# A hybrid encoder block on one core: every work buffer at a multiple of 512 bytes

## The chip, the cores and the metric

The kernel runs on one core of a Trainium2 chip. Times are device microseconds (us) of one execution. The kernel before took 1132.4 us (median of three runs, 1129.93 to 1132.73).

## What is computed

One layer over 1024 rows of 1024 numbers, all float32:

```
h = rmsnorm(x, norm1_g)
q, k, v, u = split(h @ w_in)
a = attention_mixer(q, k, v, ...)          # 8 query heads, 2 key heads, 2-D rotary positions
p = pool_mixer(u, ...)                     # four groups of 128 channels, windows 2, 4, 8, 16:
                                           #   window mean of u minus u, then a 128x128 map
x = x + concat([a, p]) @ w_out
h = rmsnorm(x, norm2_g)
x = x + (silu(h @ w_gate) * (h @ w_up)) @ w_down     # inner width 2816
```

## The kernel before

Each float32 operand of a product is split into a rounded part and the rest (`hi`, `lo`, type float32r), and a product is three passes on TensorE: hi·hi, hi·lo, lo·hi. A pass is one weight load of 128x128 (the stationary operand) and one matmul in which up to 512 columns (2048 bytes in each partition, the moving operand) stream past it.

The stages follow each other on TensorE: the input projection (line 469 for keys and values, 664 for the pooling groups, 580 for queries), the pooling groups' linear map (722), attention (scores 790, transposes of the weights 820, values 833) with the output projection between (870), then the gate and up products of the feed-forward part (1124), which take Winograd's form (seven block products instead of eight), and in the same form the down product (1397), once after every four blocks of gate and up; the last down product is plain (1349). A gate or up block is 84 matmuls, seven block products of twelve; four blocks are 336.

The order in which all engines issue is fixed before the program is built: class `Flow` plays the program with estimated costs, and a job's instruction is issued when its operands and engine are free by that estimate. Each engine then takes its own list in order. Splits and sums may fall to ScalarE (ACT), VectorE (DVE) or GpSimd (POOL), whichever `Flow.quicker` says is done first.

SBUF is laid out by tile pools, one after another. The pool `wk` has 33 work slots that hold nearly everything: transposed rows, split weights, attention weights, sums. A slot is as large as the largest tile asked of the pool. That is a pooling tile: `windows` (line 678) takes tiles of S + PAD = 1032 numbers, since eight zeros ahead of the 1024 rows of u stand for the rows before the first. So a slot is 4128 bytes, 8 x 512 + 32. In the built program the first slot starts 320 bytes past a multiple of 512, and each next slot 32 bytes further: a work tile's place modulo 512 takes all 16 multiples of 32. Behind `wk` lie `raw` (weights as loaded, 3 slots) and `ring` (split operands, 3 slots), 4096 bytes each, all at 352 modulo 512, and from the other end of SBUF the tiles `vv`, `fold`, `identr` and the pool `half`, at 480. `kT` lies at 352, the rows `qp` at 320, the float32 identity `ident` at 128. In line 1124 the stationary operand is always in `ring` and the moving one in `wk`; in line 1397 the stationary is in `ring`, and the moving one in `raw` for most steps and in `wk` for some.

The pooling window sums are made by doubling on DVE (lines 687, 690), then the mean minus u (696) and the first and last rows, whose windows are cut, apart (702, 704).

Of the kernel before, what the change touches and what calls it, by code (L numbers as in the profile page):

```python
# [41 lines left out]
AHEAD = 2  # L42
NSLOT = 33
NRAW = 3
K = {
    "pieces": 1, "groups": [[0], [1], [2, 3], [4, 5, 6, 7]], "take": [0, 3], "tables": 2, "spread": [1],
    "ahead": [22, 39], "turn_k": 40, "wq": [60], "mix": [40, 50, 0, 15], "prep_q": [20], "turn_q": [33],
# [54 lines left out]


class Nothing:
    """Stands for the machine where only the order of the work is sought."""

    def __getattr__(self, name):
        return self
# [26 lines left out]


class Flow:
    """Fixes the order in which the engines issue their instructions.

    The tensor engine's instructions come in the order of the program.  Work of the other  # L140
    engines is given as generators that yield (engine, estimated us) before each instruction,
    or a list of jobs to wait for; an instruction is issued when the estimate says that
    its engine and its operands are free by the time the tensor engine gets there."""

    LATENCY = 0.15
    COLD = 12.0
# [87 lines left out]
        held[held.index(None)] = job  # L234

    def needs(self):
        """When the tensor engine, never held up, would ask for each job."""
        for job in reversed(self.all):
            for other, before in job.waits:
                other.need = min(other.need, job.need - (job.cost - before))  # L240
        return [job.need - job.cost for job in self.all]
# [30 lines left out]
def block_kernel(  # L272
# [14 lines left out]
    pairs = ExitStack()  # L287
    ps2 = pairs.enter_context(tc.tile_pool(name="ps2", bufs=2, space=bass.MemoryType.PSUM))

    const = sb(ctx, "const")  # L290
    small = sb(ctx, "small", bufs=2)
    ident = const.tile([P, P], F32, name="ident")
    if not isinstance(nc, Nothing):
# [34 lines left out]
            nc.vector.tensor_tensor(lo, src, hi.bitcast(F32), op=ALU.subtract)  # L328

    def combine(n, dst, a, b, op):  # L330
        """dst = a op b in SBUF on whichever of DVE and Pool is done with it first"""
        way = flow.quicker(dve(n), pool(n))
        yield way
        (nc.gpsimd if way[0] == "G" else nc.vector).tensor_tensor(dst, a, b, op=op)  # L334
# [57 lines left out]
        return hs[a][h][k // 2][:, o:o + n]  # L392

    def load_w(col, n, per, apart=False):
        """W_in[:, col:col+n] as (hi, lo, job) for each k."""
        res = []
        for j in range(NK // per):
            raw, at, tok = fetch(
                lambda v: v.rearrange("p (k n) -> p k n", n=n),
                w_in2[j * per * P:(j + 1) * per * P, col:col + n].rearrange("(k p) n -> p k n", p=P))  # L400
            hi, lo = work(F32R), work(F32R)
            if not apart:
                job = consume(tok, flow.add(split(hi, lo, raw, D, both=True), at))
            for k in range(per):
                c = slice(k * n, (k + 1) * n)
                if apart:
                    job = consume(tok, flow.add(split(hi[:, c], lo[:, c], raw[:, c], n, both=True), at))
                res.append((hi[:, c], lo[:, c], job))
        return res
# [242 lines left out]

    def pool_group(g):
        wu = wus.pop(g)
        u = work(n=S + PAD)
        nc.gpsimd.memset(u[:, 0:PAD], 0.0)
        jobs = []
        for h in range(2):
            pu = bank()
            for k in range(NK):  # L660
                hi, lo, job = wu[k]
                flow.tensor(0.648, job, *[x_turned[t, k] for t in range(4 * h, 4 * h + 4)])
                for i, (a, b) in enumerate(PASSES):
                    nc.tensor.matmul(pu, (hi, lo)[a], hT(b, k, h * HALF, HALF), start=(k == 0 and i == 0), stop=(k == NK - 1 and i == 2))  # L664
                if k < NK - 1:
                    yield

            def evacuate(h, pu):
                yield [rb_jobs[h]]
                yield dve(HALF)  # L670
                nc.vector.tensor_tensor(u[:, PAD + h * HALF:PAD + (h + 1) * HALF], pu, rb[0][:, h * HALF:(h + 1) * HALF], op=ALU.mult)

            jobs.append(flow.add(evacuate(h, pu)))
            flow.hold("b1", jobs[-1])
            if h == 1:
                pooled_parts[g] = flow.add(windows(g, u, jobs))
            yield

    def windows(g, u, jobs):
        w = WINDOWS[g]  # L680
        yield jobs
        n = S + PAD
        ab = [work(n=n), work(n=n)]
        cur, step, i = u, 1, 0
        while step < w:
            yield dve(n)
            nc.vector.tensor_tensor(ab[i][:, 0:n - step], cur[:, 0:n - step], cur[:, step:n], op=ALU.add)
            if 2 * step < w:
                yield dve(1)
                nc.vector.tensor_copy(ab[i][:, n - step:n], cur[:, n - step:n])  # L690
            cur, step, i = ab[i], 2 * step, 1 - i
        hw = w // 2
        off = PAD - hw
        pooled = ab[i][:, 0:S]
        yield dve(S)
        nc.vector.scalar_tensor_tensor(pooled, cur[:, off:off + S], 1.0 / w, u[:, PAD:PAD + S], op0=ALU.mult, op1=ALU.subtract)
        for s, (c0, cn) in enumerate(((0, hw), (S - hw + 1, hw - 1))):
            if cn == 0:
                continue
            ec = small.tile([P, PAD], F32, tag="ec", name="ec")  # L700
            yield dve(1)
            nc.vector.tensor_tensor(ec[:, :cn], cur[:, off + c0:off + c0 + cn], edge[:, g, s, :cn], op=ALU.mult)
            yield dve(1)
            nc.vector.tensor_tensor(pooled[:, c0:c0 + cn], ec[:, :cn], u[:, PAD + c0:PAD + c0 + cn], op=ALU.subtract)
        ph, pl = work(F32R), work(F32R)
        us[g] = ph, pl
        yield from split(ph, pl, pooled, S, both=True)
# [143 lines left out]
    class OutProj:  # L851
# [3 lines left out]
            self.rows = rows  # L855

        def run(self, n):
            """n times the three passes of one k"""
            for _ in range(min(n, NK - self.i)):
                k = KORDER[self.i]  # L860
                if self.i == 0:
# [103 lines left out]
            x2n_job[t0 + i] = flow.add(scaled(first, i))  # L965

    def turn_h(h, k):
        """128 columns of the normalised rows of half h, transposed and split."""
        pt, name = any_bank()
        for i in range(4):  # L970
            flow.tensor(0.107, x2n_job[4 * h + i])
            nc.tensor.transpose(pt[:, i * P:(i + 1) * P], x2n[4 * h + i][:, k * P:(k + 1) * P], ident)
        dst = pieces()

        def evacuate():
            yield act(512, 0.05)
            nc.scalar.activation(dst[:, 0], pt, AF.Copy, scale=g2[:, k:k + 1])
            yield dve(512)
            nc.vector.scalar_tensor_tensor(dst[:, 1], pt, g2[:, k:k + 1], dst[:, 0].bitcast(F32), op0=ALU.mult, op1=ALU.subtract)

        h2[h, k] = dst, flow.add(evacuate())
        return pt, name, h2[h, k][1]
# [8 lines left out]
    t_split = {}  # L991

    def sums_of(i, p12, n12, job12, p22, n22, job22):
        """The sums of both halves' parts i and i + 4 that Winograd's form takes."""
        j = i + PARTS
        t1, t2, t3, t4 = (spare() for _ in range(4))
        a, b = h2[0, i][0], h2[0, j][0]
# [134 lines left out]
    wdown = {}  # L1132

    def fetch_down(f):
        """Rows of w_down for a pair whose last product takes Winograd's form."""
        t = work()
        nc.sync.dma_start(t, w_down2[f * P:(f + 1) * P, :])
        wdown[f] = t, flow.load(P * D * 4, flow.now)

    class Passed:  # L1140
        """Stands in for the reader of a slot that the tensor engine reads."""
        done, ready = False, float("inf")

    made_pair, passed = {}, {}

    def sums(p, name):
        """The sums in place that an operand of pair p needs."""
        made = made_pair.setdefault(p, {})
        if name in made:
            return made[name]  # L1150
# [32 lines left out]
    FORM = {"A11": "B11", "S1": "T1", "A12": "B21", "S2": "T2", "S3": "T3", "S4": "B22", "A22": "T4"}  # L1183

    def make_pair(p, name):
        """Both operands of one of Winograd's products of the last product, for pair p."""
        made = made_pair.setdefault(p, {})
        other = FORM[name]
        left = {"A11": (0, 0), "S1": (1, 0), "A12": (0, 1), "S2": (1, 0), "S3": (0, 0), "S4": (0, 1), "A22": (1, 1)}[name]
# [26 lines left out]
        return (x, jl), (y, jr)  # L1216

    def emit(b, q, psum, name, plus, *waits):
        """Block q of the output, plus + psum, on its way to g; the bank goes back when it is read."""
        kind, p = blocks[b]  # L1220
        f, h = 2 * p + int(q[0]) - 1, int(q[1]) - 1
        if kind == "g":
# [83 lines left out]
        users[:] = [e22, e12, emit(b, "21", b4, n4, u, j4)]  # L1306

    def plain_tile(b, f, h, *fills):
        """Tile f of block b for half h: the operands' numbers, and how many to have ready after each."""
        py, name = any_bank()  # L1310
        for i, (n, fill) in enumerate(fills):
            n, fill = n + b * len(FIRST), fill + b * len(FIRST)
# [40 lines left out]
                    split_wd(2 * p + 1, 1)  # L1353

    def into(t, c, src, op=ALU.add, in_bank=True, last=False, waits=(), n0=0, size=HALF):
        """One more term of the output's tile (t, c)."""
        cs = slice(c * HALF + n0, c * HALF + n0 + size)
        dst = qp[:, t, cs]

# [286 lines left out]
```

## Time and profile before

| | before |
|---|---|
| runs, us | 1132.73, 1132.4, 1129.93 |
| median, us | 1132.4 |
| profiled execution: first to last instruction, us | 1131.3 |
| TensorE (PE) busy, us | 1087.5 |
| weight loads (PEld) busy, us | 880.1 |
| DVE, ACT, POOL busy, us | 875.7, 454.1, 553.0 |
| granted TensorE clock, mean | 0.994 |

The profile gives one execution; its span is its whole time, 1.1 us below the median of the runs. A matmul's own duration (some 395 ns for 512 columns) is longer than the distance from one matmul's start to the next, as they are pipelined; what counts for the time is the distance, which is read from the starts of two rows, or from the chain of waits, where a row's length is the time until the next row and its x the number of matmuls.

### The profile page before, as it was taken

What the parts mean: (1) busy time and instruction counts of PE and PEld (TensorE: products, weight loads), DVE (VectorE), ACT (ScalarE), POOL (GpSimd) and SP (SyncE); (2) the same over time, 40 slices, a digit from 0 to 9 for tenths busy, and PEclk for the clock granted to TensorE, in tenths of its full rate; (3) what the DMA queues carried; (4) which work ended last, traced back from release to release, by engine and by line L of the source; (5) the groups of instructions that cost most, each with busy time, mean ns of one, the idle gap of its engine ahead of it and who ended that gap; (6) DMA issues with size and microseconds to landing.
All of it is one profiled execution on the core that took longest, in us unless ns stands there. A gap on an engine that the chain in (4) does not pass through costs nothing.

```text
span 1131.3 us, 14027 instructions
## 1 busy us (share of the span) xinstructions
PE 1087.5 (96%) x5114; PEld 880.1 (78%) x5114; DVE 875.7 (77%) x1371; ACT 454.1 (40%) x808; POOL 553.0 (49%) x442
## 2 busy tenths in 40 slices
PE   6989998999999999999899999999899989999998
PEld 6868876888888888878678877888688867887787
DVE  7888699977676765887986689658976698668985
ACT  6613367666666554522431233223322232223320
POOL 3163566522333223754862387336843485238820
PEclk9999999999999999999999999999999999999999
DMA  8112011000000001130122002310122012200113
GB/s 257 56 38 75 19 56 38 19 20 19 10 20 17 22 29 56 38 112 1 38 94 75 19 19 75 99 32 1 46 86 93 1 38 92 76 19 10 46 56 149
DMA packets 42565, 58.49 MB, mean 52 GB/s; under 512 B 4224, under 2 KB 32768, under 8 KB 42496
## 3 DMA queue, kind: packets, MB, share of 16 engines
q1 hardware_dynamic: 42496, 57.59, 15.9%
q8 instruction: 40, 0.66, 0.2%
q14 instruction: 29, 0.24, 0.1%
HBM read 53.39 MB, written 4.19 MB: 51 GB/s over the span
## 4 chain that ended last, share of the span: by engine, by line
PE 78%; DVE 15%; POOL 3%; issue 3%; ACT 1%; DMA 0%; SPq 0%; DVEq 0%; ACTq 0%; POOLq 0%
PE b L1124 36%; PE b L1397 8%; PE b L870 8%; PE b L833 5%; PE b L790 5%; PE b L820 5%; DVE wk L334 3%; PE b L664 3%; DVE silu L334 2%; DVE qp L1364 2%; PE b L1349 2%; PE b L580 2%; PE b L469 2%; POOL wk L334 1%; DVE ring L334 1%
## 5 line engine op out<-in xcount | busy, mean ns | idle before, releaser
L1124 PE MATMUL b<-wk,ring 128*128 128x512 f32 x1872 | 437.0, 395 | 1.4 <-DVE ring L321 1.4
L1124 PEld LDWEIGHTS b<-wk,ring 128*128 128x128 f32 x1872 | 351.4, 188 | 85.5 <-DVE ring L321 1.9
L1397 PE MATMUL b<-raw,ring 128*128 128x512 f32 x660 | 158.8, 395 | 8.9 <-POOL raw L334 3.6
L1397 PEld LDWEIGHTS b<-raw,ring 128*128 128x128 f32 x660 | 122.0, 188 | 44.1 <-POOL raw L334 8.5
L334 POOL TENSOR_TENSOR ring<-raw,ring 128x512 fp32r<-128x512 f32 x59 | 78.1, 1325 | 155.6 <-ACT ring L319 124.5
L809 POOL TENSOR_SCALAR wk<-wk,rsm 128x1024 f32<-128x1024 f32 x64 | 74.5, 1170 | 141.8 <-ACT wk L801 70.0
L319 ACT ACTIVATE ring<-raw 128x512 fp32r<-128x512 f32 x85 | 52.9, 630 | 211.7 <-PE b L1124 91.9
L328 DVE TENSOR_TENSOR wk<-b,wk 128x512 fp32r<-128x512 f32 (+1 forms) x160 | 101.5, 658 | 38.1 <-ACT wk L319 38.0
L319 ACT ACTIVATE wk<-b 128x512 fp32r<-128x512 f32 (+1 forms) x160 | 90.0, 575 | 80.8 <-PE b L820 60.6
L1364 DVE TENSOR_TENSOR qp<-qp,b 128x512 f32<-128x512 f32 (+1 forms) x167 | 105.7, 675 | 13.0 <-PE b L1349 9.4
L334 DVE TENSOR_TENSOR ring<-raw,ring 128x512 fp32r<-128x512 f32 x91 | 78.4, 867 | 45.4 <-POOL ring L323 23.4
L870 PE MATMUL b<-wk 128*128 128x512 f32 x384 | 102.5, 397 | 0.0
L790 PE MATMUL b<-kT,wk 128*128 128x512 f32 x256 | 89.4, 432 | 0.0
L833 PE MATMUL b<-wk,vv 128*128 128x512 f32 x256 | 82.0, 399 | 4.7 <-DVE wk L328 4.5
L319 ACT ACTIVATE ring<-silu 128x512 fp32r<-128x512 f32 x65 | 40.9, 629 | 111.0 <-PE b L1397 33.1
L870 PEld LDWEIGHTS b<-wk 128*128 128x128 f32 x384 | 70.9, 188 | 15.2
L799 DVE TENSOR_REDUCE nm<-b 128x1 f32<-128x1024 f32 x64 | 77.9, 1217 | 3.7 <-PE b L790 2.6
L334 POOL TENSOR_TENSOR wk<-wk 128x512 f32<-128x512 f32 (+3 forms) x53 | 72.6, 1384 | 15.4 <-DVE wk L1007 10.9
L334 POOL TENSOR_TENSOR ring<-silu,ring 128x512 fp32r<-128x512 f32 x45 | 60.5, 1344 | 37.4 <-ACT ring L319 37.4
L801 ACT ACTIVATE wk<-b,nm 128x1024 f32<-128x1024 f32 x64 | 71.3, 1114 | 18.2 <-DVE nm L799 17.8
L820 PE MATMUL b<-ident,wk 128*128 128x128 f32 x512 | 76.7, 272 | 0.7 <-POOL wk L809 0.7
L820 PEld LDWEIGHTS b<-ident,wk 128*128 128x128 f32 x512 | 63.7, 140 | 17.5 <-POOL wk L809 0.9
(142 smaller groups left out, 1600.5 us busy)
## 6 DMA issues: line engine op xcount, KB each, us to landing
raw<-in_w_gate_dram SPq DMA_DIRECT2D x22, 512.0 KB, 3.8
raw<-in_w_up_dram SPq DMA_DIRECT2D x22, 512.0 KB, 3.9
wk<-in_w_down_dram SPq DMA_DIRECT2D x20, 512.0 KB, 5.4
raw<-in_w_in_dram SPq DMA_DIRECT2D x10, 512.0 KB, 4.1
qp<-in_x_dram SPq DMA_DIRECT2D x8, 512.0 KB, 8.9
raw<-in_w_out_dram SPq DMA_DIRECT2D x8, 512.0 KB, 3.4
out_dram<-qp SPq DMA_DIRECT2D x15, 256.0 KB, 2.0
raw<-in_x_dram SPq DMA_DIRECT2D x14, 256.0 KB, 2.7
```

Of the source, the lines that this page charges most:

```text
L319: nc.scalar.activation(hi, src, AF.Copy)
L328: nc.vector.tensor_tensor(lo, src, hi.bitcast(F32), op=ALU.subtract)
L334: (nc.gpsimd if way[0] == "G" else nc.vector).tensor_tensor(dst, a, b, op=op)
L790: nc.tensor.matmul(s[:, c * 512:(c + 1) * 512], qT[t][0][:, h * P:(h + 1) * P], kT[:, kv, b, c * 512:(c + 1) * 512], start=(b == 0), stop= ...
L799: nc.vector.tensor_reduce(nm, s, axis=AX, op=ALU.max, negate=True)
L809: nc.gpsimd.tensor_scalar(pe, pe, rs, 1.0, op0=ALU.mult, op1=ALU.mult)
L820: nc.tensor.transpose(pt[:, j * P:(j + 1) * P], pe[:, c * P:(c + 1) * P], ident)
L833: nc.tensor.matmul(po[t, kv], vt, ps[:, b], start=(c == 0 and b == 0), stop=(c == NT - 1 and b == 1))
L870: nc.tensor.matmul(self.py, mix[self.t][a][:, k, :], wo[k][b][:, self.cs], start=(self.i == 0 and i == 0), stop=(self.i == NK - 1 and i == 2))
L1124: nc.tensor.matmul(bank_, w[0][:, a, i], x[:, b], start=(start and i == 0 and j == 0), stop=(stop and i == PARTS - 1 and j == 2))
L1364: nc.vector.tensor_tensor(dst, dst, src, op=op)
L1397: nc.tensor.matmul(banks[t][0], x[:, a, t * P:(t + 1) * P], y[:, b], start=(i == 0 and j == 0), stop=(i == 1 and j == 2))
```

## The change

The pooling tiles lose their zero margin: `windows` now sums over the 1024 rows alone, and the sums of the first rows, which need the margin, are made apart on POOL in small tiles `le` of 24 numbers (`first_sums`). So a work slot is 4096 bytes. Two fillers that nothing reads (`rim` of 480 bytes at the far end of SBUF, `gap` of 320 bytes at its start) shift what follows them. In the built program all of `wk`, `raw`, `ring`, `qp`, `kT`, `vv`, `half`, `fold` and `identr` then start at multiples of 512. `ident`, the moving operand of the float32 transposes (lines 453, 820 and 972 of before), does not: it goes from 128 to 448 modulo 512. Docstrings go too; lines move by 3 to 20.

```diff
+RIM, GAP = 120, 80
...
+    sb(ctx, "rim", side="right").tile([P, RIM], F32, name="rim")
     const = sb(ctx, "const")
+    const.tile([P, GAP], F32, name="gap")
...
-        u = work(n=S + PAD)
-        nc.gpsimd.memset(u[:, 0:PAD], 0.0)
+        u = work()
...
+    def first_sums(g, u, le, job):
+
+        w = WINDOWS[g]
+        yield [job]
+        yield pool(1)
+        nc.gpsimd.memset(le[0][:, 0:PAD], 0.0)
+        yield pool(1)
+        nc.gpsimd.tensor_copy(le[0][:, PAD:], u[:, 0:2 * PAD])
+        step, i, n = 1, 0, 3 * PAD
+        while step < w:
+            n -= step
+            yield pool(1)
+            nc.gpsimd.tensor_tensor(le[1 - i][:, 0:n], le[i][:, 0:n], le[i][:, step:n + step], op=ALU.add)
+            step, i = 2 * step, 1 - i
+
     def windows(g, u, jobs):
         w = WINDOWS[g]
+        hw = w // 2
+        le = [small.tile([P, 3 * PAD], F32, tag=f"le{i}", name="le") for i in range(2)]
+        edged = flow.add(first_sums(g, u, le, jobs[0]))
         yield jobs
-        n = S + PAD
-        ab = [work(n=n), work(n=n)]
+        ab = [work(), work()]
...
-        pooled = ab[i][:, 0:S]
+        pooled = ab[i]
         yield dve(S)
-        nc.vector.scalar_tensor_tensor(pooled, cur[:, off:off + S], 1.0 / w, u[:, PAD:PAD + S], op0=ALU.mult, op1=ALU.subtract)
-        for s, (c0, cn) in enumerate(((0, hw), (S - hw + 1, hw - 1))):
+        nc.vector.scalar_tensor_tensor(pooled[:, hw:S], cur[:, 0:S - hw], 1.0 / w, u[:, hw:S], op0=ALU.mult, op1=ALU.subtract)
+        first = le[w.bit_length() % 2 == 0][:, PAD - hw:PAD]
+        for s, (c0, cn, src) in enumerate(((0, hw, first), (S - hw + 1, hw - 1, cur[:, S - w + 1:S - hw]))):
...
+            if s == 0:
+                yield [edged]
             yield dve(1)
-            nc.vector.tensor_tensor(ec[:, :cn], cur[:, off + c0:off + c0 + cn], edge[:, g, s, :cn], op=ALU.mult)
+            nc.vector.tensor_tensor(ec[:, :cn], src, edge[:, g, s, :cn], op=ALU.mult)
```

TensorE's list is the same as before, instruction by instruction, and so is SP's. The other lists differ in the pooling stage alone. On DVE, between the evacuation of the third bank of the pooling products and that of the fifth, the list before was (L671 evacuates a bank, L687 is a doubling, L334 the `lo` part of the first group's result):

```order
L702 TENSOR_TENSOR ec<-wk,pk 128x8
L671 TENSOR_TENSOR wk<-b_775,wk 128x512
L704 TENSOR_TENSOR wk<-ec,wk 128x8
L702 TENSOR_TENSOR ec<-wk,pk 128x7
L704 TENSOR_TENSOR wk<-ec,wk 128x7
L334 TENSOR_TENSOR wk<-wk 128x1024
L671 TENSOR_TENSOR wk<-b_825,wk 128x512
L687 TENSOR_TENSOR wk<-wk 128x1031
L690 COPY wk<-wk 128x1
L687 TENSOR_TENSOR wk<-wk 128x1030
L690 COPY wk<-wk 128x2
L671 TENSOR_TENSOR wk<-b_873,wk 128x512
```

In the changed kernel the same place reads (L673 evacuates a bank, L706 is a doubling, `le` is POOL's small tile):

```order
L673 TENSOR_TENSOR wk<-b_780,wk 128x512
L722 TENSOR_TENSOR ec<-le,pk 128x8
L724 TENSOR_TENSOR wk<-ec,wk 128x8
L673 TENSOR_TENSOR wk<-b_830,wk 128x512
L722 TENSOR_TENSOR ec<-wk,pk 128x7
L724 TENSOR_TENSOR wk<-ec,wk 128x7
L706 TENSOR_TENSOR wk<-wk 128x1023
L709 COPY wk<-wk 128x1
L706 TENSOR_TENSOR wk<-wk 128x1022
L709 COPY wk<-wk 128x2
L706 TENSOR_TENSOR wk<-wk 128x1020
L673 TENSOR_TENSOR wk<-b_874,wk 128x512
```

The first group's `lo` has left DVE, one more doubling stands ahead of the fifth bank's evacuation, and the first edge row now waits for POOL. On POOL, at the same time, the list before was (L656 is the margin of u, L323 a `hi`):

```order
L334 TENSOR_TENSOR wk<-raw,wk 128x1024
L334 TENSOR_TENSOR wk<-qp,wk 128x2x128 x3
L656 MEMSET wk 128x8
L323 TENSOR_SCALAR wk<-raw 128x1024
L334 TENSOR_TENSOR wk<-raw,wk 128x1024
L323 TENSOR_SCALAR wk<-wk 128x1024
```

In the changed kernel, from the copy of the first group's first rows on:

```order
L688 COPY le<-wk 128x16
L337 TENSOR_TENSOR wk<-qp,wk 128x2x128
L693 TENSOR_TENSOR le<-le 128x23
L693 TENSOR_TENSOR le<-le 128x21
L693 TENSOR_TENSOR le<-le 128x17
L693 TENSOR_TENSOR le<-le 128x9
L686 MEMSET le 128x8
L688 COPY le<-wk 128x16
L693 TENSOR_TENSOR le<-le 128x23
L693 TENSOR_TENSOR le<-le 128x21
L693 TENSOR_TENSOR le<-le 128x17
L337 TENSOR_TENSOR wk<-wk 128x1024
```

The small sums of two groups stand there, and behind them the first group's `lo`; the split of loaded weights that POOL made here (L323, 128x1024) has gone to ACT.

## Rows read from the trace of the kernel before

**Rows 1.** The page, busy time: engine, us, share of span, instructions; and granted clock.
```profile
PE 1087.5 (96%) x5114; PEld 880.1 (78%) x5114; DVE 875.7 (77%) x1371; ACT 454.1 (40%) x808; POOL 553.0 (49%) x442
PEclk9999999999999999999999999999999999999999
```

**Rows 2.** The page, chain that ended last, by line.
```profile
PE b L1124 36%; PE b L1397 8%; PE b L870 8%; PE b L833 5%; PE b L790 5%; PE b L820 5%; DVE wk L334 3%; PE b L664 3%; DVE silu L334 2%; DVE qp L1364 2%; PE b L1349 2%; PE b L580 2%; PE b L469 2%; POOL wk L334 1%; DVE ring L334 1%
```

**Rows 3.** That chain in order of time, feed-forward part: start us, length us, what.
```profile
495.32 36.03 PE b L1124 x154
...
575.70 78.02 PE b L1124 x336
653.72 9.56 PE b L1397 x42
...
688.86 9.32 PE b L1397 x39
...
1067.00 38.99 PE b L1124 x168
1106.00 22.33 PE b L1349 x102
```

**Rows 4.** Timeline of PE, end of two down products: start, busy us, line.
```profile
572.82 2.88 PE L1397 MATMUL b<-wk,ring 128*128 128x512 f32 x12
575.54 0.84 PE L1124 MATMUL b<-wk,ring 128*128 128x512 f32 x3
...
695.21 2.98 PE L1397 MATMUL b<-wk,ring 128*128 128x512 f32 x12
698.02 2.26 PE L1124 MATMUL b<-wk,ring 128*128 128x512 f32 x9
```

**Rows 5.** The chain in order of time, before the feed-forward part.
```profile
96.28 9.07 PE b L664 x39
...
119.24 11.15 PE b L580 x48
...
201.16 1.39 PE b L870 x6
```

**Rows 6.** Groups by line and shape: count, busy us, mean ns, idle before.
```profile
L1364 DVE TENSOR_TENSOR qp<-qp,b 128x512 f32<-128x512 f32 x165 | 104.8, 678 | 12.8 <-PE b L1349 9.1 <-PE b L1397 3.3
L328 DVE TENSOR_TENSOR wk<-b,wk 128x512 fp32r<-128x512 f32 x144 | 96.0, 685 | 37.4 <-ACT wk L319 37.4
L334 POOL TENSOR_TENSOR wk<-wk 128x1024 fp32r<-128x1024 f32 x1 | 2.4, 2405 | 3.8 <-ACT wk L319 3.8
```

**Rows 7.** Timeline of PE, DVE and POOL in the pooling stage.
```profile
82.85 0.75 PE L557 MATMUL b<-identr,wk 128*128 128x128 f32 x4 [4.54 <-DVE wk L671]
...
75.39 1.23 DVE L334 TENSOR_TENSOR wk<-wk 128x1024 fp32r<-128x1024 f32 x1 [1.19 <-ACT wk L319]
82.11 0.68 DVE L671 TENSOR_TENSOR wk<-b,wk 128x512 f32<-128x512 f32 x1
82.72 1.21 DVE L687 TENSOR_TENSOR wk<-wk 128x1028 f32<-128x1028 f32 x1
...
59.21 0.10 POOL L656 MEMSET wk<- 128x8 f32 x1
59.96 0.46 POOL L334 TENSOR_TENSOR qp<-qp,wk 128x128 f32<-128x128 f32 x1
68.78 3.31 POOL L334 TENSOR_TENSOR wk<-qp,wk 128x256 fp32r<-128x256 f32 x3
```

**Rows 8.** Busy time by stretch: PE, PEld, DVE, ACT, POOL, granted clock, DMA.
```profile
78.00:83.00 5.00, 0.46 (x3) 0.16 (x2) 4.97 (x6) 0.00 (x0) 3.03 (x1) 0.76 0.17 20
83.00:88.00 5.00, 5.00 (x21) 3.93 (x22) 3.97 (x8) 1.79 (x3) 0.80 (x1) 0.56 0.22 85
...
575.00:653.00 78.00, 78.00 (x338) 63.15 (x337) 54.60 (x82) 18.92 (x31) 28.09 (x23) 1.00 0.21 67
653.00:663.00 10.00, 10.00 (x46) 8.26 (x45) 7.30 (x11) 4.27 (x8) 7.96 (x7) 1.00 0.00 0
```

More of the change, by code (lines that the diff above doesn't have):

```diff
@@ L670, in evacuate @@
                 yield dve(HALF)
-                nc.vector.tensor_tensor(u[:, PAD + h * HALF:PAD + (h + 1) * HALF], pu, rb[0][:, h * HALF:(h + 1) * HALF], op=ALU.mult)
+                nc.vector.tensor_tensor(u[:, h * HALF:(h + 1) * HALF], pu, rb[0][:, h * HALF:(h + 1) * HALF], op=ALU.mult)
             jobs.append(flow.add(evacuate(h, pu)))
@@ L677, in pool_group @@
             yield
+    def first_sums(g, u, le, job):
[11 more added lines that the diff above has]
+            step, i = 2 * step, 1 - i
     def windows(g, u, jobs):
         w = WINDOWS[g]
+        hw = w // 2
+        le = [small.tile([P, 3 * PAD], F32, tag=f"le{i}", name="le") for i in range(2)]
+        edged = flow.add(first_sums(g, u, le, jobs[0]))
         yield jobs
-        n = S + PAD
-        ab = [work(n=n), work(n=n)]
+        ab = [work(), work()]
         cur, step, i = u, 1, 0
         while step < w:
-            yield dve(n)
-            nc.vector.tensor_tensor(ab[i][:, 0:n - step], cur[:, 0:n - step], cur[:, step:n], op=ALU.add)
+            yield dve(S)
+            nc.vector.tensor_tensor(ab[i][:, 0:S - step], cur[:, 0:S - step], cur[:, step:S], op=ALU.add)
             if 2 * step < w:
                 yield dve(1)
-                nc.vector.tensor_copy(ab[i][:, n - step:n], cur[:, n - step:n])
+                nc.vector.tensor_copy(ab[i][:, S - step:S], cur[:, S - step:S])
             cur, step, i = ab[i], 2 * step, 1 - i
-        hw = w // 2
-        off = PAD - hw
-        pooled = ab[i][:, 0:S]
+        pooled = ab[i]
         yield dve(S)
-        nc.vector.scalar_tensor_tensor(pooled, cur[:, off:off + S], 1.0 / w, u[:, PAD:PAD + S], op0=ALU.mult, op1=ALU.subtract)
-        for s, (c0, cn) in enumerate(((0, hw), (S - hw + 1, hw - 1))):
+        nc.vector.scalar_tensor_tensor(pooled[:, hw:S], cur[:, 0:S - hw], 1.0 / w, u[:, hw:S], op0=ALU.mult, op1=ALU.subtract)
+        first = le[w.bit_length() % 2 == 0][:, PAD - hw:PAD]
+        for s, (c0, cn, src) in enumerate(((0, hw, first), (S - hw + 1, hw - 1, cur[:, S - w + 1:S - hw]))):
             if cn == 0:
@@ L700, in windows @@
             ec = small.tile([P, PAD], F32, tag="ec", name="ec")
+            if s == 0:
+                yield [edged]
             yield dve(1)
-            nc.vector.tensor_tensor(ec[:, :cn], cur[:, off + c0:off + c0 + cn], edge[:, g, s, :cn], op=ALU.mult)
+            nc.vector.tensor_tensor(ec[:, :cn], src, edge[:, g, s, :cn], op=ALU.mult)
             yield dve(1)
-            nc.vector.tensor_tensor(pooled[:, c0:c0 + cn], ec[:, :cn], u[:, PAD + c0:PAD + c0 + cn], op=ALU.subtract)
+            nc.vector.tensor_tensor(pooled[:, c0:c0 + cn], ec[:, :cn], u[:, c0:c0 + cn], op=ALU.subtract)
         ph, pl = work(F32R), work(F32R)
```

## The prediction

> **What bounds the kernel now.** First the page's busy times and the clock: PE is busy 96% of the span and its granted clock is 9 tenths or more in every slice [rows 1]. [...] So the time is mostly PE's own stream of matmuls, not waiting and not a low clock. Second the chain that ended last by line: matmul lines lead it, the gate and up products (L1124) alone with 36% [rows 2]. Third the same chain in order of time, which gives the pace. A stretch of 336 matmuls of L1124 takes 78.02 us, 232.2 ns from start to start [rows 3], and PE is busy all through it while DVE is busy 54.60 of 78.00 us and POOL 28.09 [rows 8]: PE alone sets this stretch. There are four such stretches, all within 0.03 us of this one, and shorter ones of 154 and 168.
>
> The down product (L1397) right behind runs 42 matmuls in 9.56 us, 227.6 ns each [rows 3], at the same clock of 1.00 [rows 8], with the same shapes, three passes and a weight load for each. What differs is where the operands lie: in those 42 the moving operand is in `raw` and the stationary one in `ring`, both at 352 modulo 512; in L1124 the moving one comes from a `wk` slot at any of 16 offsets.
>
> The cleanest contrast is inside one line. Twelve matmuls at the end of a down product, moving operand in `wk`, stationary in `ring`: in the first product they take 575.54 - 572.82 = 2.72 us (226.7 ns each), in the second 698.02 - 695.21 = 2.81 us (234.2 ns) [rows 4]. In the built program the first one's moving slot is at 96 modulo 512, which is 256 away from the stationary's 352; the second one's is at 192, which is 160 away. The three later down products alternate in slot and in length alike. I take from this that the pace depends on the distance between the two operands' addresses modulo 512 (or 256): 227 ns where it is zero, about 232 on average over all offsets.
>
> **What the change adds, removes and moves.** (a) Feed-forward blocks. Every moving and stationary operand now lies at 0, so the distance is zero throughout. I take 227.0 ns, between the 226.7 of the twelve and the 227.6 of the 42, which hold a few slower ones behind L1124. A stretch of 336: 336 x 0.2270 = 76.3 us, a gain of 1.75 us, four times 7.0. The 154 in 36.03 us: to 34.96, 1.1. The 168 in 38.99: to 38.14, 0.85. Together 8.9 us. DVE's slack in these stretches (30% of 78 us) covers the faster demand for operands; without it the 1.75 us would be handed to a wait.
>
> (b) The down products already run at 227.6 where they read `raw`. Between their first 42 and last 39 matmuls the chain goes through DVE and POOL for some 25 us (688.86 less 663.28), which does not change. The last 39 take 9.32 us [rows 3]; at 227.0 they take 8.85. Five times 0.47 is 2.3; some of it is a wait behind DVE, and where the twelve are at 96 there is nothing to gain, so 1.2.
>
> (c) The plain last product: 102 matmuls, 12 of them half as wide, in 22.33 us [rows 3], so 96 full ones at 232.6 ns; at 227.0, 21.8: gain 0.5.
>
> (d) Before the feed-forward part: L870 six in 1.39 us (231.7 ns), L580 48 in 11.15 us (232.3), L664 39 in 9.07 us (232.6) [rows 5]. L580 and L664 have 192 matmuls each: 192 x 5.3 ns = 1.0 us each; L580 counts in full, L664 for half, as the chain goes partly through DVE there. Attention has 896 matmuls of 512 columns (256 + 256 + 384) at some 5 ns: 4.5 us in full. But there they come in pieces of two to six between transposes, whose moving operand `ident` stays off the grid (at 448), and the slower matmuls behind L1124 in (b) suggest that the good pace is reached only after a few. I take half, 2.2. Together 3.7.
>
> (e) The pooling stage. PE waits there 4.54 us at L557 for DVE to empty a bank (L671, 82.11 us) [rows 7]. Ahead of that evacuation DVE loses the first group's `lo` and the wait before it (1.23 + 1.19 us) and gains one doubling (1.21) [rows 7]. It may also wait for POOL's `le`: behind three splits (3.31 us) stand a copy and four additions of 9 to 23 columns, each between 0.10 us (a memset of 8) and 0.46 us (128 columns) [rows 7], so ready 0 to 1.5 us after DVE gets there. The first group's `lo` now takes POOL's 2.4 us [rows 6] instead of DVE's 1.2, so PE waits already at the map of that group (L722), and less at L557. Bounds: a gain of 2.4 us (all that leaves DVE) and a loss of 1.5; I take a gain of 0.7. The clock fell here behind the idle time, to 0.76 and 0.56 in the ten us from 78 [rows 8]; two shorter waits instead of one may keep it up, which I do not count.
>
> (f) Nothing else. DVE's time does not hang on the address: 678 ns at the `qp` slots, 685 over all `wk` offsets [rows 6]. The fillers issue nothing. The DMA list is the same.
>
> Sum: 8.9 + 1.2 + 0.5 + 3.7 + 0.7 = 15.0 us. From the profiled 1131.3 that gives 1116.3; the median of the runs is 1.1 above that profile, so **1117**.
>
> [...]
>
> **The rivals.** (1) No change: the pace differs between lines and slots for another reason (the order of products, writes of other engines into the same slots), not the distance. For it: six matmuls of L870, whose two operands lie in `wk` at many distances, keep a rather even 231.7 ns. Against it: the alternation in [rows 4]. Then only (e) is left: 1131.3 - 0.7 + 1.1 = 1131.7. (2) Slower: the pace hangs on each operand's own offset, and 0 is one of the bad ones; nothing in the trace has both operands at 0 for long. Then the stream locks in at the pace of the bad slots, 234.2 ns [rows 4], instead of the mean of 232.2. The four stretches, the 154 and the 168 (1666 matmuls) lose 2.0 ns each, 3.3 us; the down products' matmuls that run at 227 now (42 and about 24 on the chain, five times) 6.6 ns each, 2.2 us; the rest of about 1370 matmuls 2 to 3 ns, 3.0 us: together 8.5 less 0.7, 1140. It decides from a pace of about 232.5 ns on. (3) A larger gain: zero distance and a 512-byte start together cut more than `raw` and `ring` at 352 show. [...] (4) That the words don't hold in full: `ident` is not on the grid. The transposes of four take the same place in the chain whatever slot they read, so this costs what (d) already leaves out.
>
> **How the numbers follow.** My forecast 0.68, no change 0.13, slower 0.11, the larger gain 0.08. The forecast's own range is 1110 (attention in full, the pooling stage at its good end, the end of the down products in full) to 1124 (half of (a), nothing in attention). For 8 in 10 the range goes from 1108, which leaves out most of the larger gain, to 1133, which takes in no change and leaves out slower. A measurement of this kernel can tell about 0.3% (3.4 us) from no change: faster by more 0.76, within 0.13, slower 0.11.
>
> **What would show it.** Right: the chain's pieces of 336 at about 76.3 us; the last twelve of L1397 alike in all down products, 2.72 us; the plain last product at 21.8. In attention a piece of six L870 at 1.36 would mean the full gain there, 1.39 none. In the pooling stage a wait at L722's counterpart ahead of the one at L557's, together no more than 5 us. Wrong: pieces of 336 at 78.0 (no change) or 78.7 (slower); or at 76.3 with new waits of PE for `ring` ahead of the down products, if DVE does not keep up.

## The result and the profile after

The changed kernel takes 1124.95 us (median of 9 runs, 1121.60 to 1126.29), the kernel before 1132.21 beside it (9 runs, 1126.96 to 1133.97). The ratio is 0.9943, with a 95% interval of 0.9927 to 0.9959: 7.3 us faster in the medians, where 15 were forecast. The direction and the range hold; the size is half.

The page of the changed kernel, busy time and granted clock, to be read beside [rows 1]:

```profile
PE 1075.4 (96%) x5114; PEld 878.7 (78%) x5114; DVE 871.3 (78%) x1371; ACT 455.6 (41%) x810; POOL 555.2 (50%) x454
PEclk9999999999999999999999999999999999999999
```

PE has the same 5114 matmuls and is busy 12.1 us less. The profiled execution has a span of 1120.9 us, 10.4 less than before's, and its run took 1122.64: some 1.7 us lie around a span (a span is not a run's whole time, in the kernel before neither), and this run is 2.3 under its kernel's median, while before's profiled span of 1131.3 belongs to a run of some 1133, 0.8 above its median. So what the two traces show adds up to 10.4, and the medians show 7.3.

The chain in order of time, as [rows 3] (start us, length us, what; L1144 was L1124, L1417 was L1397, L1369 was L1349):

```profile
120.14 10.89 PE b L583 x48
...
495.26 35.21 PE b L1144 x154
530.47 9.53 PE b L1417 x42
565.60 9.12 PE b L1417 x39
574.71 76.19 PE b L1144 x336
650.91 9.53 PE b L1417 x42
...
926.84 10.71 PE b L1417 x39
937.55 76.16 PE b L1144 x336
...
1057.93 38.08 PE b L1144 x168
1096.01 21.84 PE b L1369 x102
```

A stretch of 336 takes 76.16 to 76.19 us, 226.7 ns for a matmul, where it took 78.02; the plain last product is at 21.84. One piece of 39 takes 10.71: the granted clock from 925 to 940 us is 0.89 in the mean.

The timeline of PE at the end of the first two down products (start, busy us, line), as [rows 4]:

```profile
571.83 2.88 PE L1417 MATMUL b<-wk,ring 128*128 128x512 f32 x12
574.55 5.63 PE L1144 MATMUL b<-wk,ring 128*128 128x512 f32 x24
...
692.28 2.88 PE L1417 MATMUL b<-wk,ring 128*128 128x512 f32 x12
695.00 5.18 PE L1144 MATMUL b<-wk,ring 128*128 128x512 f32 x22
```

574.55 - 571.83 and 695.00 - 692.28 are both 2.72: the alternation of [rows 4] is gone.

Attention, the chain (as the last line of [rows 5]; L890 was L870), and the pooling stage, timelines of PE, DVE and POOL (as [rows 7]; L742 was L722, L560 was L557, L673 was L671):

```profile
201.77 1.39 PE b L890 x6
```

```profile
76.29 0.51 PE L742 MATMUL b<-wk 128*128 128x512 f32 x1 [0.34 <-ACT wk L322]
79.79 1.83 PE L742 MATMUL b<-wk 128*128 128x512 f32 x5 [2.99 <-POOL wk L337]
83.79 0.75 PE L560 MATMUL b<-identr,wk 128*128 128x128 f32 x4 [2.17 <-DVE wk L673]
...
76.31 1.22 DVE L706 TENSOR_TENSOR wk<-wk 128x1022 f32<-128x1022 f32 x1
77.45 2.30 DVE L709 COPY wk<-wk 128x2 f32<-128x2 f32 x1
79.79 3.35 DVE L706 TENSOR_TENSOR wk<-wk 128x1020 f32<-128x1020 f32 x1
83.06 0.68 DVE L673 TENSOR_TENSOR wk<-b,wk 128x512 f32<-128x512 f32 x1
...
76.31 3.42 POOL L337 TENSOR_TENSOR wk<-wk 128x1024 fp32r<-128x1024 f32 x1 [1.45 <-ACT wk L322]
79.70 2.36 POOL L337 TENSOR_TENSOR wk<-raw,wk 128x1024 fp32r<-128x1024 f32 x1
```

Attention keeps its 1.39. PE waits in the pooling stage 0.34 + 2.99 + 2.17 = 5.50 us instead of 4.54. Later, among the query products, it waits once where the kernel before did not, behind a split of POOL that took 2.98 us (108.87 to 111.85) with a pooling sum of DVE beside it until 109.60:

```profile
111.89 6.88 PE L583 MATMUL b<-wk 128*128 128x512 f32 x29 [0.58 <-POOL le L686]
```

Where the 10.4 us of the traces arose is read from the start of the same matmul in both, since PE's list is the same. After is 0.57 us ahead at 57 us (PE's waits up to 57 us, more than half of them for the input, add up to 9.8 us in before and 9.1 in after), 0.93 ahead at 74 us, 0.94 behind at 83 us: the pooling stage cost 1.9 us there, of which 0.2 come back by 87 us. Behind that the gain of the query products and the loss at 111.89 (0.20 behind ahead of it, 0.93 after it) nearly cancel out. It is 0.60 behind at 212 us and 0.29 behind at 430 us, so attention gave 0.3. From there to the end it gains 10.8, and stands 10.5 ahead. Behind 57 us the granted clock is alike in both, 0.79 from 74 to 90 us and 0.89 from 925 to 940 us:

```profile
74.00:90.00 16.00, 10.50 (x48) 7.50 (x46) 13.80 (x18) 4.40 (x6) 8.95 (x10) 0.79 0.12 34
925.00:940.00 15.00, 13.67 (x54) 10.85 (x53) 12.88 (x18) 4.79 (x9) 13.00 (x10) 0.89 0.26 90
```

(Busy time by stretch in after, columns as [rows 8].) So 10.5 - 0.6 = 9.9 us of the gain in the traces have nothing to do with the start or the clock.

### The profile page after: what moved, and what is told of

It reads as the page before. It is cut to its first block, busy times and chain, and to the rows that moved or that the text cites. A ratio compares the mean times of both kernels' runs of the same rounds, so it can differ in the third digit from the quotient of the medians.

```text
span 1120.9 us, 14036 instructions
## 1 busy us (share of the span) xinstructions
PE 1075.4 (96%) x5114; PEld 878.7 (78%) x5114; DVE 871.3 (78%) x1371; ACT 455.6 (41%) x810; POOL 555.2 (50%) x454
## 4 chain that ended last, share of the span: by engine, by line
PE 72%; DVE 14%; POOL 4%; issue 3%; ACT 1%; DMA 0%; DVEq 0%; ACTq 0%; POOLq 0%
PE b L1144 36%; PE b L1417 8%; PE b L890 8%; PE b L853 5%; PE b L810 5%; PE b L840 5%; DVE wk L337 2%; DVE silu L337 2%; DVE qp L1384 2%; POOL wk L337 2%; PE b L1369 2%; PE b L583 2%; DVE ring L337 1%; DVE wk L1297 1%; DVE qp L337 1%
## 5 line engine op out<-in xcount | busy, mean ns | idle before, releaser
L1144 PE MATMUL b<-wk,ring 128*128 128x512 f32 x1872 | 427.1, 389 | 1.8 <-DVE ring L324 1.8
L1144 PEld LDWEIGHTS b<-wk,ring 128*128 128x128 f32 x1872 | 350.7, 188 | 76.7 <-DVE ring L324 2.2
L1417 PE MATMUL b<-raw,ring 128*128 128x512 f32 x660 | 158.6, 394 | 8.9 <-POOL raw L337 3.6
L1417 PEld LDWEIGHTS b<-raw,ring 128*128 128x128 f32 x660 | 121.9, 188 | 43.9 <-POOL raw L337 8.4
L890 PE MATMUL b<-wk 128*128 128x512 f32 x384 | 102.1, 396 | 0.0
L337 POOL TENSOR_TENSOR wk<-wk 128x512 f32<-128x512 f32 (+3 forms) x55 | 78.3, 1437 | 26.1 <-ACT wk L322 14.8
L853 PE MATMUL b<-wk,vv 128*128 128x512 f32 x256 | 81.8, 398 | 4.7 <-DVE wk L331 4.5
L890 PEld LDWEIGHTS b<-wk 128*128 128x128 f32 x384 | 70.8, 188 | 15.2
```

The source lines that it names most:

```text
L853: nc.tensor.matmul(po[t, kv], vt, ps[:, b], start=(c == 0 and b == 0), stop=(c == NT - 1 and b == 1))
L890: nc.tensor.matmul(self.py, mix[self.t][a][:, k, :], wo[k][b][:, self.cs], start=(self.i == 0 and i == 0), stop=(self.i == NK - 1 and i == 2))
L1144: nc.tensor.matmul(bank_, w[0][:, a, i], x[:, b], start=(start and i == 0 and j == 0), stop=(stop and i == PARTS - 1 and j == 2))
L1417: nc.tensor.matmul(banks[t][0], x[:, a, t * P:(t + 1) * P], y[:, b], start=(i == 0 and j == 0), stop=(i == 1 and j == 2))
```

## The experiments

Theory: the pace of a stream of 512-column matmuls depends on the distance between the moving and the stationary operand, modulo 256 or 512. Rivals: it depends on each operand's own offset; or the gain came from the new pooling code, or from the order of the work.

**Without the fillers.**

```diff
-    sb(ctx, "rim", side="right").tile([P, RIM], F32, name="rim")
...
-    const.tile([P, GAP], F32, name="gap")
```

> The changed kernel without its two fillers: work, raw and ring slots all lie at 192 modulo 512, so the distance between moving and stationary operand is zero but neither is at a multiple of 512. Distance theory: the gate and up stretches of 336 matmuls take 76.2 us as in the changed kernel, the time is within 2 us of it (1125). Theory of the own offset (each operand must start at a multiple of 512): the stretches go back to about 78 us, the time to about 1132 to 1135.

Measured: 1126.48 us (4 runs), ratio 0.9958 (0.9941 to 0.9974). The chain:

```profile
575.30 76.18 PE b L1142 x336
...
1098.08 22.35 PE b L1367 x102
```

The stretch of 336, whose operands now lie at 192 modulo 512 both, keeps the good pace; the plain last product, whose two operands no longer lie at the same place (480 and 192), is back at before's 22.33. With the run after, this shows that the distance counts, not the grid.

**The stationary operand moved against the moving one.** A filler between `wk` and what follows it, of 32, 64, 128, 160 or 256 bytes; `rim` shrinks by as much, so that the tiles at the far end move too. PE's list stays the same. The edit for 32 bytes:

```diff
-RIM, GAP = 120, 80
+RIM, GAP, STEP = 112, 80, 8
...
+    sb(ctx, "step").tile([P, STEP], F32, name="step")
```

> The changed kernel with raw and ring 32 bytes further, so that in the gate and up products the stationary operand lies 32 past the moving one (0) modulo 512. Distance theory: about 233 ns from start to start, as the down product's matmuls of before at that distance, so a stretch of 336 takes 78.3 us; the steps of the down product that read raw stay at 227. Own-offset theory with the moving operand deciding: 76.2 us, since it still lies at 0.

> Raw and ring 160 bytes further. Distance theory: about 234.5 ns, the pace of the bad twelve of before (distance 160), a stretch of 336 in 78.8 us, some 10 us slower in all than the changed kernel. Own offset of the moving operand: 76.2 us.

> Raw and ring 256 bytes further. If the distance counts modulo 256, as the good twelve of before suggest: 226.8 ns and 76.2 us, as at distance 0. If it counts modulo 512: about 232 ns, 78 us. Own offset of the moving operand: 76.2 us, so this run alone does not tell that one apart.

> As the steps of 32, 160 and 256: raw, ring, kT and the right-hand tiles lie 128 bytes further than wk, modulo 512, by a filler of 128 bytes between them; nothing else changes. The runs so far leave open whether the distance counts modulo 64, 128 or 256, since 32 and 160 are odd multiples of 32 and 256 is zero by all three. Modulo 256 (my reading): a stretch of 336 L1144 takes 78.4 us as at 32 and 160, the span is some 1137. Modulo 128 or 64: 76.2 us, the span some 1122.

> The same with 64 bytes. Modulo 256 or 128: a stretch of 336 L1144 takes 78.4 us, the span is some 1137. Modulo 64: 76.2 us, the span some 1122. If 64 is fast and 128 slow or the other way round, the pace is no matter of a single modulus.

Measured, one run each, beside 1132.1 to 1132.2 for the kernel before. The first stretch of 336 and the piece of 42 behind it, whose operands (`raw` and `ring`) moved together, from the chains; step of 32:

```profile
579.85 78.40 PE b L1145 x336
658.25 9.56 PE b L1418 x42
```

Step of 64:

```profile
579.85 78.40 PE b L1145 x336
```

Step of 128:

```profile
576.72 78.40 PE b L1145 x336
```

Step of 160:

```profile
582.02 78.40 PE b L1145 x336
```

Step of 256:

```profile
576.46 76.19 PE b L1145 x336
652.64 9.53 PE b L1418 x42
```

| step, bytes | 336 of L1145, us | a matmul, ns | time, us |
|---|---|---|---|
| 0 (after) | 76.19 | 226.8 | 1124.95 |
| 32 | 78.40 | 233.3 | 1137.48 |
| 64 | 78.40 | 233.3 | 1137.58 |
| 128 | 78.40 | 233.3 | 1134.25 |
| 160 | 78.40 | 233.3 | 1139.93 |
| 256 | 76.19 | 226.8 | 1124.38 |

The difference between before and after in the feed-forward part appears and disappears with the place of the tiles behind `wk`. Zero and 256 are good, every other step tried is bad by the same 6.5 ns: a modulus of 256, which leaves 512, 128 and 64 out. The 78.8 us expected at 160 did not come; 160 is no worse than 32. Before's 232.2 is then close to a mean of one good offset in eight and seven bad ones, 226.8 / 8 + 233.3 x 7/8 = 232.5, an estimate, as 96, 192 and 224 were not tried.

**The new pooling code alone.** After's code with the slots 4128 bytes apart again and no fillers. To make room, the small tiles `le` and `ec` have one buffer instead of two; the lists of PE, DVE and POOL are those of after.

```diff
-        ab = [work(), work()]
+        ab = [work(n=S + PAD)[:, 0:S], work()]
...
-    sb(ctx, "rim", side="right").tile([P, RIM], F32, name="rim")
...
-    const.tile([P, GAP], F32, name="gap")
```

> The changed pooling code alone: the instruction lists are those of the changed kernel, but the work slots are 4128 bytes apart again, so that moving and stationary operands lie at mixed distances as before. Theory that the pooling stage took back what is missing from the forecast: the stretches of 336 take 78.0 us as before, queries begin 1.5 to 3 us later than before, and the time is 3 to 5 us above the kernel before (1135 to 1137), with a lower mean granted clock than before's 0.994. Rival, that the pooling code costs nothing and the missing gain lies elsewhere: within 1 us of the kernel before (1132).

Measured: 1137.17 us (12 runs, 1131.40 to 1141.39), ratio 1.0048 (1.0031 to 1.0066), 4.9 us slower than before. PE in the pooling stage, and the chain:

```profile
76.15 1.43 PE L740 MATMUL b<-wk 128*128 128x512 f32 x5 [1.94 <-POOL wk L336]
81.32 0.75 PE L558 MATMUL b<-identr,wk 128*128 128x128 f32 x4 [3.74 <-DVE wk L671]
...
577.05 78.21 PE b L1142 x336
```

1.94 + 3.74 = 5.68 us of waits instead of 4.54. That and slightly worse offsets (four times 78.21 - 78.02) explain about 2 of the 4.9 us. The rest goes with the clock. The mean granted clock of before's runs is 0.994 (38 runs), of this kernel's 0.992 (12), of after's 0.991 (9), and over all runs of this study the time of a kernel's runs follows it by 1.06 us for each 0.001, with 0.8 us of scatter. Read at the same clock of 0.994, before takes 1132.45 (20 runs), this kernel 1134.45 (2 runs) and after 1121.60 (one run); at 0.991 this kernel takes 1137.09 (3 runs) and after 1124.99 (4), at 0.989 1140.48 (5) and 1126.09 (2). So from this kernel's offsets to a distance of zero the addresses are worth 12 to 14 us, and the pooling code by itself costs some 1 by its waits and 3 by the clock.

**`ident` on the grid too.** Every matmul operand then starts at a multiple of 512.

```diff
-RIM, GAP = 120, 80
+RIM, GAP = 120, 96
...
-    warm = const.tile([P, 1], F32, name="warm")
+    ssq1 = const.tile([P, NT], F32, name="ssq1")
+    warm = ssq1[:, 0:1]
...
-            ec = small.tile([P, PAD], F32, tag="ec", name="ec")
+            ec = small.tile([P, PAD], F32, tag="ec", name="ec", bufs=1)
```

> The changed kernel with ident, too, at a multiple of 512, so that all 5112 matmuls have both operands at 0. If ident's place kept attention from its gain: the pieces of six output-projection matmuls go from 1.39 to 1.36 us, attention (160 to 440 us) loses 3 to 4.5 us, time about 1121. Rival, that the transposes between break the pace wherever their operands lie: pieces stay at 1.38 to 1.39 us and the time stays at 1125.

Measured: 1125.22 us (6 runs), ratio 0.9944 (0.9932 to 0.9956), as after. Two pieces of attention in the chain:

```profile
203.39 1.39 PE b L890 x6
208.19 1.38 PE b L890 x6
```

The place of `ident` is not what holds attention at 231 ns.

**No transposes in attention.** The four transposes of a step become two ordinary matmuls of 512 columns; the attention weights aren't transposed.

```diff
-            nc.tensor.transpose(pt[:, j * P:(j + 1) * P], pe[:, c * P:(c + 1) * P], ident)
+            if j % 2:
+                nc.tensor.matmul(pt, pe[:, c * P:(c + 1) * P], kT[:, kv, 0, 0:512], start=(j == 1), stop=(j == 3))
...
-        pe = work()
+        pe = work(F32R)
```

> After's code, but in attention the four float32 transposes of a step (L840, 128 of these groups) are replaced by two ordinary matmuls of 512 columns that read the attention weights as the stationary operand and kT as the moving one, both at a multiple of 512. The attention weights are not transposed here, so the output is not the reference's; PE does about as much work (2 x 227 for 4 x 109 ns, less 85 ns at each change of kind). Theory that transposes between break the pace: with none left, the output projection (L891) and the values (L854) run at 226.8 to 228 ns; a piece of six L891 takes 1.36 us or less instead of 1.39. Theory that pieces of two to six are too short whatever stands between (each change of bank and operand costs): they stay at 230.5 to 232. The time falls in any case by some 128 x (436 + 85 - 454) ns = 8.6 us at most, if DVE and POOL keep up; by the first theory by 3 us more.

Measured: 1123.28 us (one run, before 1132.22 beside it). The chain in attention:

```profile
197.50 1.36 PE b L891 x6
...
200.22 0.68 PE b L891 x3
```

41 of the 46 pieces of six between 190 and 437 us take 1.36 us, 226.7 ns each; in after 29 of 46 take 1.39 and none 1.36. The pieces are as short as before and change bank and operands as often, so shortness is not the reason: the transposes between them are. Whether it is their type (float32), their 128 columns or the transposing itself, this run does not tell. In after mostly 4 to 10 matmuls stand between two groups of transposes. The first one takes 316 ns (median, to the next start); then those of L853 take 228 to 233 in places three to seven and 227 in the ninth, and those of L890 are mixed: 233 and 236 in the third and fourth, 226 in the fifth, 231 in the sixth and seventh, 227 in the eighth. My price of the transposes in the expectation was wrong, and with it the time: a group of four takes 355 ns and delays the next matmul by 85, so two matmuls (454 ns) save nothing.

**Four other pooling stages.** The first three lie on after's grid; the fourth does not, as is said below. The first group's `lo` back on DVE:

```diff
-        yield from split(ph, pl, pooled, S, both=True)
+        if g == order[0]:
+            yield from split(ph, pl, pooled, S)
+        else:
+            yield from split(ph, pl, pooled, S, both=True)
```

> The changed kernel, but the low part of the first pooling group is made on DVE instead of where the planner puts it (POOL, 3.42 us in the profile of the changed kernel). If that wait is the pooling stage's loss: PE's wait of 2.99 us for POOL at the first group's map goes, queries begin 1 to 3 us earlier, time 1121 to 1124. Rival, that DVE is the limit there and the work only comes back to it: queries begin at the same time, 1125.

The small sums on DVE (their memset and copy move as well):

```diff
...
-            yield pool(1)
-            nc.gpsimd.tensor_tensor(le[1 - i][:, 0:n], le[i][:, 0:n], le[i][:, step:n + step], op=ALU.add)
+            yield dve(1)
+            nc.vector.tensor_tensor(le[1 - i][:, 0:n], le[i][:, 0:n], le[i][:, step:n + step], op=ALU.add)
```

> The changed kernel with the small sums of the first rows on DVE instead of POOL (14 more DVE instructions of some 0.15 us each, POOL's 21 gone); the first group's low part stays on POOL. If the small sums on POOL are the loss: POOL's low part ends 1 to 2 us earlier, time 1122 to 1124. Rival, that the low part on POOL is the loss by itself: 1125 or slightly more.

Both edits together:

> After's code with both repairs of the pooling stage together: the small sums of the first rows on DVE instead of POOL, and the first group's lo on DVE behind ACT's hi, as before. POOL then has nothing of the pooling stage that it had not before. If the lost time of that stage is POOL's place in it, the two waits of PE shrink to one at L560's counterpart of at most 4.8 us, the granted clock's mean comes back to that of before (0.994 instead of 0.991), and the time is 1121.5 (ratio 0.9905). If the lower clock goes with the stage whatever engine makes the sums, the clock stays near 0.991 and the time at 1124 to 1125 (ratio 0.993).

And no sums of the first rows at all:

```diff
-        edged = flow.add(first_sums(g, u, le, jobs[0]))
...
-        first = le[w.bit_length() % 2 == 0][:, PAD - hw:PAD]
+        first = cur[:, 0:hw]
...
-            if s == 0:
-                yield [edged]
```

> After's code without the sums of the first rows: no le, no wait of DVE for it; the first rows of each pooling group read a part of the doubled sums that is not theirs, so their values are not the reference's. The grid is as in after. If POOL's small sums and the wait for them cost the pooling stage its time, PE's waits there fall to before's 4.5 us or less and the clock to before's 0.994: 1121 (ratio 0.990). If the loss comes from the rest of the new pooling code (the lo of the first group on POOL, one more doubling ahead of the bank), the waits stay at some 5.2 us and the time at 1124.5 (ratio 0.993).

| | time, us (runs) | ratio (95%) | PE waits in the stage, us | mean clock of the runs |
|---|---|---|---|---|
| before | 1132.21 (9) | 1 | 4.54 | 0.994 |
| after | 1124.95 (9) | 0.9943 (0.9927 to 0.9959) | 5.50 | 0.991 |
| `lo` on DVE | 1123.02 (6) | 0.9926 (0.9907 to 0.9946) | 5.20 | 0.992 |
| sums on DVE | 1124.49 (6) | 0.9939 (0.9926 to 0.9951) | 5.78 | 0.991 |
| both | 1128.31 (6) | 0.9948 (0.9929 to 0.9967) | 4.44 | 0.9905 |
| no first sums | 1129.00 (8) | 0.9968 (0.9948 to 0.9987) | 5.84 | 0.989 |

PE's timeline, with `lo` on DVE:

```profile
76.71 1.43 PE L745 MATMUL b<-wk 128*128 128x512 f32 x5 [1.37 <-DVE wk L709]
81.97 0.74 PE L560 MATMUL b<-identr,wk 128*128 128x128 f32 x4 [3.83 <-DVE wk L673]
```

With the sums on DVE:

```profile
79.96 1.88 PE L742 MATMUL b<-wk 128*128 128x512 f32 x5 [2.41 <-POOL wk L337]
85.20 0.74 PE L560 MATMUL b<-identr,wk 128*128 128x128 f32 x4 [3.37 <-DVE wk L673]
```

With both on DVE, PE's timeline and the stretch by busy time:

```profile
73.30 7.57 PE L666 MATMUL b<-wk 128*128 128x512 f32 x25 [2.07 <-POOL wk L337]
81.66 1.45 PE L745 MATMUL b<-wk 128*128 128x512 f32 x5 [0.56 <-DVE wk L709]
84.92 0.75 PE L560 MATMUL b<-identr,wk 128*128 128x128 f32 x4 [1.81 <-DVE wk L673]
...
74.00:90.00 16.00, 13.62 (x50) 10.38 (x49) 14.33 (x27) 2.80 (x4) 5.04 (x4) 0.71 0.22 66
```

With no first sums, PE's timeline (two more waits are of 0.19 and 0.15), and from the chain the end of the first down product and the plain last product:

```profile
80.28 0.75 PE L560 MATMUL b<-identr,wk 128*128 128x128 f32 x4 [5.50 <-DVE wk L673]
...
564.49 10.74 PE b L1413 x39
...
1098.45 22.38 PE b L1365 x102
```

This last run is not on after's grid, against its expectation. The `le` tiles it leaves out took 384 bytes ahead of `qp` and `wk`; in the built program `wk`, `raw`, `ring`, `qp` and `kT` lie at 128 modulo 512, and `vv`, `half`, `fold` and `identr` at 0. So the values (moving operand in `wk`, stationary in `vv`) and most of the plain last product are at a distance of 128, and the last product takes 22.38 us, before's pace.

Nor do the waits alone tell what a stage costs. PE's list has the same order in all six kernels, so the same matmul can be compared, each against the kernel before. From 65 us to the first transposes behind the long wait (82.85 in before) after loses 1.7 us, `lo` on DVE 0.8, the sums on DVE 2.0, both 1.9, no first sums 1.6: up to there `lo` on POOL is half of the loss, and the small sums are not its cause. From 65 to 131 us the losses, the clock's part in them, are 1.4, 0.9, 2.4, 3.3 and 0.3: behind the long wait the sums do cost something, since without them the wait at 111.89 is gone too. With both on DVE the waits of the stage fall to 4.44, but they come in three, the clock between 74 and 90 us is granted at 0.71 instead of 0.79, and 1.15 us of waiting follow at 121 us. Two or three shorter waits didn't keep the clock up.

The times don't follow these losses, because of the clock in the feed-forward part. Where it falls at the end of a down product, the last 39 matmuls take 10.7 to 10.8 us instead of 9.1 to 9.3. In the profiled executions that happens once in before (the fourth down product), in after and with the sums on DVE, and three times (the first, third and fifth) with `lo` on DVE, with both and with no first sums. So the medians of 1128 and 1129 don't show that these two pooling stages are worse by themselves. `lo` on DVE has the lowest median, but its interval overlaps after's. The time of about 1121 that the last two expectations held for possible did not come in the medians, and even at a clock of 0.994 both on DVE takes 1123.4 (2 runs).

## Why the prediction was right in kind and twice too large

**(a) and (c): right; (b): half.** The four stretches gained 1.83 to 1.89 us each (1.75 forecast), the 154 gained 0.82 (1.1), the 168 0.91 (0.85), together 9.2 for 8.9. The plain last product gained 0.49 against 0.5. The ends of the down products gained 0.6 together, and the 42 ahead of them 0.1, against 1.2: the 9.32 that the prediction took for all five was the slowest of the four at full clock, as before's chain has it:

```profile
566.47 9.23 PE b L1397 x39
...
933.75 10.84 PE b L1397 x39
```

(The fourth, 10.84, is before's fall of the clock.) In after the four at full clock take 9.12 to 9.15. The five steps, in which only the stationary operand moves, and the run without fillers, in which both lie at 192, show together that the distance sets the pace and not one operand's own place. Rival (1), no change, falls at 76.19; rival (2), an offset of 0 being bad, falls with after itself, and with the run without fillers, as fast at 192 as at 0; rival (3), a still faster pace, falls at 226.8. No run shows the size of that gain, from which the 1108 of the range is taken; the fastest pace of a stretch here is 226.7.

Here the same list of instructions takes 76.19 or 78.40 us for 336 matmuls by the place of the stationary operand alone. Where inside the chip the 6.5 ns are lost, no run here shows.

**(d): the step "I take half, 2.2" for attention failed.** It came to 0.3 (from 0.60 behind at 212 us to 0.29 behind at 430 us). The prediction had seen that the good pace may be reached only after a few matmuls, but took half of the gain all the same; the 4 to 10 matmuls that mostly stand between two groups of transposes are too few, and the run with none shows it: without transposes the same pieces run at 226.7. In the part without transposes the pace came as forecast, 48 of L580's successor in 10.89 instead of 11.15, but most of the 1.5 us given to it went to two waits that the prediction did not have: 0.7 at 111.89 and, at the first transposes of the queries (L782, before L762), 0.73 for DVE instead of 0.28.

**(e): the step "I take a gain of 0.7" had the wrong sign.** By the traces the stage cost 1.7 us up to 87 us, beyond the lower bound of 1.5, and its waits came to 5.50 us, more than the 5 that the prediction gave as a sign. The prediction gave the first group's `lo` POOL's 2.4 us of [rows 6] and left DVE's doublings at 1.21. Both come from places where the other engine did little (POOL's at 113.56 us with 0.9 us of DVE's work beside it, DVE's at 82.72 with POOL idle until 87.20); here the two meet. In after, POOL's `lo` and two doublings' work on DVE take turns: POOL's 3.42 holds a doubling of 1.22 first; then DVE's copy of two columns ends at 79.75, when POOL's `lo` ends (79.73), after 2.30 us (before's copy of two columns took 0.16, at 82.04, with POOL idle); then the next doubling, 3.35, ends 1.1 us after POOL's next split at 82.06. Before had one such long meeting in this place (a doubling of 3.19 at 78.93), after has two. So each engine's instruction grew beside the other's: POOL's `lo` from 2.40 us [rows 6] to 3.42, DVE's copy from 0.16 to 2.30. By what means, no run here shows. `lo` on DVE takes 0.9 of the 1.7 back.

**Not in the sum: the clock.** The prediction named the clock's fall behind the wait of [rows 8] and thought that two shorter waits may keep it up, which it did not count; a further fall was not in its bounds. Over the runs the mean clock fell from 0.994 to 0.991, 3.4 us by 1.06 us for each 0.001. The 9.9 us that the traces show behind 57 us, pooling stage included, less 3.4 of the clock are 6.5; 7.3 were measured, and the 0.8 between is no more than single executions scatter. The forecast's 15.0 lost 1.9 to attention, 2.4 to the pooling stage (1.7 lost for 0.7 gained), some 1.2 to the two waits behind it, 0.5 to (b) and 3.4 to the clock. That leaves 5.6 of the 7.3 measured. Of the rest 0.3 lie in (a) and 0.3 in the first 84 matmuls of L1124, which the sum did not have; 1.1 are not accounted for, as each part is read from one execution. The run of the new pooling code alone shows that this code takes the clock most of that way (0.992). Where the clock is lost differs between executions: the two profiles behind 57 us have it alike, so the fall that the runs show can't be placed in them. With `lo` on DVE it falls at the end of the first down product and not of the second, at the same work:

```profile
560.00:580.00 20.00, 17.98 (x70) 14.14 (x71) 17.84 (x25) 7.29 (x14) 15.21 (x12) 0.91 0.22 79
680.00:700.00 20.00, 17.94 (x77) 13.84 (x76) 19.46 (x25) 7.60 (x13) 17.27 (x13) 1.00 0.29 102
```

(Busy time by stretch, columns as [rows 8]: clock 0.91 and 1.00.) What in the pooling stage decides over falls so far behind it stays open; the cause of these 3.4 us is not shown, only that they come with the new pooling code.

## What to carry to other kernels

Where TensorE is the bound and its matmuls follow each other without a break, look at the addresses: compare the same line at two places in the trace, and give both operands of a pass the same place modulo 256 bytes (0 and 256 apart took 226.8 ns a matmul; 32, 64, 128 and 160 apart 233.3). Only the difference counts (76.18 us for 336 with both at 192, 76.19 with both at 0), so equal strides and equal starts do it, without a grid from zero. Expect little of it where transposes come every few matmuls (0.3 us of 4.5 here), and price the code that makes room for it by the rows of engines that will really meet: here the edit that freed 32 bytes a slot took back some five of the twelve microseconds that the addresses gave.

## What the runs showed of the hardware

- A stream of 512-column float32r matmuls runs at 226.8 ns with the two operands 0 or 256 bytes apart modulo 512 (336 in 76.19 us), and at 233.3 ns at distances of 32, 64, 128 and 160, alike (78.40 us).
- Behind transposes the good pace is not back at once: in L853 the median is 233 ns at the third matmul and 227 at the ninth. Behind a group of float32 transposes the first float32r matmul takes 316 ns to the next start, some 85 more than those behind it.
- DVE's copy of two columns took 2.30 us beside POOL's subtraction of 1024 columns, against 0.16 us for the same copy in the kernel before, with POOL idle.
- Time and mean granted clock of a run of this kernel go together, 1.06 us for 0.001 with 0.8 us of scatter, so kernels are best compared at equal clocks; a fall at the end of a down product costs 1.6 us (39 matmuls in 10.71 us against 9.12 in after).
